# One shift row in the attention, the closing norm on VectorE, output weights loaded two ahead, and a new order for the start of the kernel

## The chip, the cores and the metric

One core of a Trainium2 chip runs the kernel. The time is that of one execution on the device in microseconds (us), from the first to the last instruction with what lies around them. Five engines work beside each other, each in the order of its own queue: PE (TensorE: matmuls and transposes; PEld are its weight loads), DVE (VectorE), ACT (ScalarE), POOL (GpSimd) and SP (SyncE, which here only issues transfers between HBM and the on-chip memory). Matmul results go to PSUM banks, everything else lives in SBUF tiles of 128 partitions. Before and after are compared by the median of several executions; one further execution was recorded by the profiler.

## The reference, cut to what matters

One layer, batch 1, 2048 positions, width 1024: an adaptive layer norm, an input projection, two branches (a gated linear recurrence and a forgetting attention of 8 heads of width 64), an output projection and a closing layer norm on the residual.

```python
mod = silu(c) @ w_ada + b_ada;  shift, scale, gate = split(mod, 3)
h = layer_norm(x) * (1 + scale) + shift
xr, zr, q, k, v, za, fl = split(h @ w_in)        # 6 of width 512, fl of width 8
y_r = rg_lru(causal_conv(xr))                    # gates by block matmuls, then a scan over positions
y_r = rms_norm(y_r, norm_lru) * silu(zr)
d = cumsum(log_sigmoid(fl + b_fgate))            # per head
s = q @ k.T / 8 + d[query] - d[key]              # causal
y_a = rms_norm(softmax(s) @ v, norm_attn) * silu(za)
y = concat(y_r, y_a) @ w_out
out = layer_norm(2 ** 0.25 * x + gate * y) * ln_gain + ln_bias
```

## The kernel before, in words

**Numbers.** Most operands are written as a sum of two f16 tiles (a high part, rounded on ACT, and the rest, on DVE or POOL), and a product is three f16 matmuls. The scales of these splits come from the largest absolute value of a tensor: `all_max` transposes column maxima on PE (`pam`), reduces them on DVE and spreads the result with a second small matmul. Every matmul is issued by the helper `mm` and therefore carries line L93; the tiles tell them apart.

**Input passes.** Positions are taken in four chunks of 512 (four tiles of 128). `load_x` loads a chunk, `norm_tile` normalises a tile: statistics and a few small steps on DVE (L236 to L244, one power on POOL), then the scaling in two halves on ACT (L266) and POOL (L268). *Pass 0* works through chunk 0 in eight steps k, one for each 128 of the width. In a step `scale_col` loads 128 columns of `w_ada` (`wadab`) and forms eight column matmuls with the activated `c` (`psc`), which give the scale of these 128 features; `load_w32` loads the matching rows of `w_in` (`wrow`) and rounds them (ACT L644, POOL L646); `make_h32` transposes the normalised x (`ptr`) and forms h in a high and a low part (ACT L380, DVE L381); `xr32` is twelve matmuls 128x512 into the four banks `pj` of the recurrence's input. *Pass 1* does the same with chunk 1, whose weights are there already, and beside it finds the scales for these weights (`col_max`, `xmax_fin`), splits them for f16 (`split_T`, tiles `wT`) and finds the shift of the adaptive norm (`wsh`, `va`, `pada`). *Pass 2* and *pass 3* take chunks 2 and 3 with the f16 weights (`make_hk`, `finish_h`, tiles `hf` and `hT`), add the shift's share to the earlier chunks (`xr_shift`: 16 small matmuls `pcj` for each of four column groups), and pass 3 prepares the weights of V (`vf_gen`: maxima, scales `vfr`, tiles `wN` and `wf`).

**Middle.** Then come V, the keys, the recurrence, the gates z and a, and the decay (`decay_gen`), each as matmuls over all chunks with element work on the other engines.

**Attention.** For each chunk of queries and each head (32 items) an item first finds a bound of the scores: matmuls `pmx` of the key rows kb (64 features, two constant rows, two rows of the decay, 68 in all) with the query rows qb, row maxima `mc` on DVE (L1259), a maximum over key blocks `mrow` (L1263). From it comes the shift of the query: L1267 writes `trow` in f32, L1268 rounds it into the f16 tile `Z`, L1269 writes the rest into the next column. PE transposes `Z` into `pzt` (66 rows), ACT copies the two rows to qb. Then for each block of keys: scores `pst` (two matmuls), exponent on ACT (L1290), split of the result into two f16 tiles (ACT L1292, then POOL L1294 or DVE L1296: `ph`), and the product with V into `acc`.

**Output.** `wout_gen` prepares the output weights beside the attention: it loads 128 rows (`woraw`), POOL multiplies them by the gate row `gbc` (L1003, 128x1024), ACT and DVE split them; one load is in flight ahead of the one at work. `out_gen` forms `pout` for a tile of positions whose attention is done, DVE adds the residual (`xres`, L1468), and `ln_gen` closes the tile: statistics on DVE, one scaling on ACT (L1385), gain and bias on POOL (L1387, L1388). The sixteenth tile has its own path (`out_last`, L1418 to L1429), which does gain and bias in four steps of 128x512 on DVE.

**What sets the order.** Each of these parts is a Python generator; the places of their `yield`s, `tick()` and `flush()` interleave them by hand. A scheduler then orders each engine's queue when the kernel is built; `tc.issue_after(ins)` adds an edge that it must keep. Buffers come from pools with fixed counts (`r4` eight of 4 KB, `t2` ten of 2 KB), so a load waits until the tile that held its buffer has been read.

Of the kernel before, what the change touches and what calls it, by code (L numbers as in the profile page):

```python
# [19 lines left out]
P = 128  # L20
# [18 lines left out]
def hybrid_mixer(  # L39
# [66 lines left out]
    kb = dr.tile([H, 68, S], F16, name="kb", tag="kb")  # L106
# [27 lines left out]
    def load_cols(parts, name):  # L134
        n = sum(k for _, k in parts)
        rows = t2([n, P], f"r_{name}")
        o = 0
        for ap, k in parts:
            flat = ap[0] if len(ap.shape) == 2 else ap[0].rearrange("k n -> (k n)")
            nc.scalar.dma_start(rows[o:o + k, :], flat.rearrange("(a b) -> a b", b=P))  # L140
# [53 lines left out]
    def pj_bank():  # L194
# [52 lines left out]
    def load_x(ci):  # L247
        xs = []
        for i in range(4):
# [5 lines left out]
            else:  # L255
                hv = [t2([P, CH], f"xt{g}") for g in range(2)]
                for g in range(2):
                    nc.sync.dma_start(hv[g], x[t * P:(t + 1) * P, g * CH:(g + 1) * CH])
# [86 lines left out]
    def split_h(ci, k, hf):  # L345
        a = nc.scalar.copy(hT(k, 0, ci), hf).ins
        nc.vector.tensor_tensor(hT(k, 1, ci), hf, hT(k, 0, ci), ALU.subtract)  # L347
# [316 lines left out]
    def wmax_fin():  # L664
        yield
        yield
        am = yield from all_max(wam, NW)
# [30 lines left out]
    def vf_gen(raws, fraw):  # L698
# [16 lines left out]
        nc.scalar.activation(wf[:, :, 0:H], fraw, AF.Copy, scale=rec[:, 1:2])  # L715
        nc.vector.scalar_tensor_tensor(wf[:, :, H:2 * H], fraw, rec[:, 1:2], wf[:, :, 0:H], ALU.mult, ALU.subtract)
# [15 lines left out]

    pss = [bank(t, "pj") for t in "AAAO"]
    for k in range(KT + 2):
# [12 lines left out]
        if k > 1:  # L747
            xr32(pss, 0, k - 2)
    xr32_out(pss, 0)
    pss = [bank(t, "pj") for t in "BBAA"]  # L750
    xam = cst([P, 4, KT], "xam")
# [11 lines left out]
    wu = []  # L763
    for k in range(KT + 2):
# [10 lines left out]
        if k == 4:  # L775
            chains.append(xmax_fin())
        if 2 <= k < 2 + 4:
            xraw.append(load_raw(P * len(xraw)))
        if k == 4:
            for g in range(2):  # L780
                nc.vector.tensor_tensor(va[g], va[g], pa[g], ALU.add)
        if k > 1:
            xr32(pss, 1, k - 2)
            tick()
        if k == 5:
# [10 lines left out]
            for j in range(4):  # L796
                wu.append((split_T(xraw[j], xrec[:, j:j + 1]), xun[:, j:j + 1]))
            norm_x(xs2, (1, 1, 1, 1,))
            last["pow2"] = last["pow"]
# [33 lines left out]
    new_h(3)  # L833
    for k in range(KT + 1):
# [11 lines left out]
        if k == 3:  # L846
            cs = [xr_shift(j) for j in range(4)]
        tick()
    flush()
# [6 lines left out]
    load_gates()  # L856
# [10 lines left out]
    nc.vector.memset(crow, RS)  # L867
    nc.scalar.dma_start(kb[:, DH:DH + 2, :].rearrange("h a s -> a h s"), crow.unsqueeze(1).broadcast_to([2, H, S]))
    QB = [cst([68, CH], f"qb{i}", F16) for i in range(4)]
    Z = [cst([P, 4, 68], f"Z{i}", F16) for i in range(4)]  # L870
    for q in QB:
        nc.scalar.dma_start(q[66:68, :], crow[:, 0:CH])
# [69 lines left out]
    def gate_gen():  # L942
# [7 lines left out]
        for k in range(KT):  # L950
# [5 lines left out]
            else:  # L956
                nc.gpsimd.tensor_tensor(out=acc, in0=acc, in1=w, op=ALU.add)
# [17 lines left out]
    def gate_fin(cols):  # L975
        yield
# [7 lines left out]
    def wout_gen():  # L984
# [15 lines left out]
        def wo_raw(k):  # L1000
            raw = r4([P, D], "woraw")
            nc.sync.dma_start(raw, w_out_v[k])
            nc.gpsimd.tensor_tensor(out=raw, in0=raw, in1=gbc, op=ALU.mult)  # L1003
            return raw

        nxt = wo_raw(0)
        yield
        for k in range(KT):
            raw = nxt
            if k + 1 < KT:  # L1010
                nxt = wo_raw(k + 1)
            w = wh([P, 2, D], "wo") if k < KT - 1 else r4([P, 2, D], "wo", F16)
            for n in range(2):
                sl = slice(n * CH, (n + 1) * CH)
                split_out(w[:, 0, sl], w[:, 1, sl], raw[:, sl], so[:, k:k + 1])
                yield
# [68 lines left out]
    def decay_gen():  # L1085
# [8 lines left out]
        yield  # L1094
        WT = t2([P, 2, H, TT], "WT")
# [28 lines left out]
        for h in range(H):  # L1124
            for a in range(2):
                nc.sync.dma_start(kb[h, DH + 2 + a, :].rearrange("(t p) -> t p", p=P), ndr[h * TT:(h + 1) * TT, a, :])
# [104 lines left out]
    def maxpass(ci, h, res):  # L1231
# [10 lines left out]
        nc.sync.dma_start(kk[0:68, 1, 0:nk], kb[h, :, 0:nk])  # L1242
# [3 lines left out]
        nc.gpsimd.memset(qb[DH:DH + 2, :], 0.0)  # L1246
# [3 lines left out]
        for i in range(4):  # L1250
            nk = (4 * ci + i + 1) * P
            for b in range(ci + 1):
# [3 lines left out]
                mm(ps[:, 0:w], qb[:, i * P:(i + 1) * P], kk[0:68, 1, b * CH:b * CH + w], True, not end)  # L1256
# [9 lines left out]
        t = sm([P, 4], "trow")  # L1266
        nc.vector.tensor_scalar(t, m, -1.0 / RS, ndc[:, ci, h:h + 1], ALU.mult, ALU.add)  # L1267
        nc.vector.tensor_copy(z[:, :, DH], t)  # L1268
        nc.vector.tensor_tensor(z[:, :, DH + 1], t, z[:, :, DH], ALU.subtract)  # L1269
# [349 lines left out]
```

## Time and profile before

| | |
|---|---|
| median of 3 runs | 1215.45 us (1214.27 to 1218.1) |
| profiled execution | 1211.64 us |
| its span, first to last instruction | 1209.9 us |
| mean granted TensorE clock | 0.966 |
| HBM read / written | 97.66 MB / 31.59 MB |

A row of the timeline gives start and length in us, engine, line, operation, output <- inputs, shape, count, and in brackets how long the engine had been idle and what ended that. In the groups the numbers behind a bar are busy us in all and mean ns of one. PSUM tiles begin with p (`pj`, `pst`, `pmx`, `pout`).

### The profile page before, as it was taken

The numbers are of one execution on the slowest core, as the hardware profiler recorded it, in microseconds if no ns is written. First come the engines' busy times: TensorE is split into PE (matmuls) and PEld (weight loads), VectorE is DVE, ScalarE is ACT, GpSimd is POOL, SyncE is SP. The second block draws the span as 40 slices with busy tenths as digits, with TensorE's granted clock in tenths as the row PEclk, the third lists the DMA queues.
The fourth block names the chain that finished last, engine by engine and source line by source line (L and its number), as shares of the span: only waits on it lengthen the run. The fifth ranks groups of instructions, "written<-read, shape, count | busy, mean of one in ns | idle before, by whom it ended". The sixth has DMA issues, their size and how long they took to land. (4 is left out here: it accounts for less than half of the span.)

```text
span 1209.9 us, 20217 instructions
## 1 busy us (share of the span) xinstructions
PE 1111.2 (92%) x7467; PEld 622.8 (51%) x7467; DVE 767.7 (63%) x1435; ACT 719.6 (59%) x1244; POOL 686.0 (57%) x670
## 2 busy tenths in 40 slices
PE   6997899999999899999979979989999989999787
PEld 6874444454444444434445545555565555565444
DVE  4378775766668953664396544576677677667534
ACT  3437545564758412623375657577888688888841
POOL 5715532444554300830277645687788689887854
PEclk9998989999999999999979989989999999999899
DMA  9653046221225712754063344222332233221001
GB/s 296 208 151 123 1 118 189 71 64 33 70 70 141 242 55 70 260 160 140 26 205 114 95 129 123 87 93 86 101 94 90 76 103 106 78 89 46 18 27 70
DMA packets 110248, 130.56 MB, mean 108 GB/s; under 512 B 10086, under 2 KB 79318, under 8 KB 110150
## 3 DMA queue, kind: packets, MB, share of 16 engines
q1 hardware_dynamic: 109840, 129.17, 35.0%
q8 instruction: 58, 0.95, 0.3%
q14 instruction: 40, 0.33, 0.1%
q10 hardware_dynamic: 310, 0.12, 0.0%
HBM read 97.66 MB, written 31.59 MB: 107 GB/s over the span
## 5 line engine op out<-in xcount | busy, mean ns | idle before, releaser
L93 PE MATMUL pj<-hT,wT 128*128 128x512 f16 x1440 | 324.4, 383 | 4.1 <-DVE hT L347 1.7
L1294 POOL TENSOR_TENSOR ph<-pf,ph 128x512 f16<-128x512 f32 (+2 forms) x240 | 260.5, 1100 | 67.4 <-ACT ph L1292 62.6
L93 PEld LDWEIGHTS <-wT 128*128 128x128 f16 x1792 | 169.2, 99 | 208.6 <-issue 21.6
L1259 DVE TENSOR_REDUCE mc<-pmx 128x1 f32<-128x512 f32 (+2 forms) x320 | 184.8, 603 | 114.2 <-PE pmx L93 110.0
L1290 ACT ACTIVATE pf<-pst,bias 128x512 f32<-128x512 f32 (+1 forms) x320 | 194.7, 634 | 66.4 <-PE pst L93 58.8
L1292 ACT CAST ph<-pf 128x512 f16<-128x512 f32 (+1 forms) x320 | 171.7, 569 | 20.1 <-PE acc L93 15.9
L93 PE MATMUL acc<-V,ph 128*128 128x129 f16 (+1 forms) x2176 | 158.6, 210 | 22.0 <-POOL ph L1294 14.6
L93 PEld LDWEIGHTS <-ph 128*128 128x128 f16 x2176 | 124.1, 99 | 80.6 <-POOL ph L1294 22.1
L93 PE MATMUL pst<-qs,kk 128*128 128x512 f16 (+1 forms) x320 | 114.3, 360 | 2.0 <-DVE mc L1259 1.3
L93 PE MATMUL pst<-qb,kk 66*128 66x512 f16 (+1 forms) x320 | 112.8, 362 | 0.2
L93 PE MATMUL pmx<-kk,qb 68*128 68x512 f16 (+2 forms) x320 | 105.0, 357 | 7.4 <-DMA kk<-kb 3.8
L93 PE MATMUL pout<-wo,yT 128*128 128x512 f16 (+1 forms) x396 | 95.7, 372 | 1.5 <-ACT yT L1370 1.5
L93 PE MATMUL pout<-wo,yr 128*128 128x512 f16 (+1 forms) x396 | 94.1, 381 | 2.8 <-DVE zs L1369 2.7
L93 PE MATMUL pj<-wN,hT 128*128 128x512 f16 x384 | 89.5, 378 | 0.2 <-ACT XL L814 0.2
L1188 POOL TENSOR_TENSOR XL<-XL,szr 128x512 f32<-128x512 f32 x16 | 24.3, 1522 | 114.7 <-ACT szr L1185 114.7
L1296 DVE TENSOR_TENSOR ph<-pf,ph 128x512 f16<-128x512 f32 (+1 forms) x80 | 64.3, 804 | 33.8 <-ACT ph L1292 33.2
L93 PEld LDWEIGHTS <-kk 66*128 66x128 f16 (+1 forms) x640 | 55.1, 100 | 34.5 <-issue 11.6
L93 PE MATMUL pq<-hT,wT 128*128 128x512 f16 x288 | 67.0, 379 | 2.8 <-DVE qhl L881 2.8
L93 PEld LDWEIGHTS <-hT 128*128 128x128 f16 x640 | 44.5, 97 | 48.3 <-issue 3.6
L93 PEld LDWEIGHTS <-yr 128*128 128x128 f16 x396 | 38.3, 100 | 42.8 <-issue 8.0
L93 PEld LDWEIGHTS <-yT 128*128 128x128 f16 x396 | 37.5, 98 | 39.4 <-ACT yT L1370 1.7
L483 POOL TENSOR_TENSOR xl<-xc,xh 128x512 fp32r<-128x512 f32 x16 | 24.4, 1532 | 57.8 <-ACT xh L481 47.0
(307 smaller groups left out, 1846.0 us busy)
## 6 DMA issues: line engine op xcount, KB each, us to landing
wraw<-in_w_in_dram SPq DMA_DIRECT2D x40, 512.0 KB
woraw<-in_w_out_dram SPq DMA_DIRECT2D x16, 512.0 KB
xres<-in_x_dram SPq DMA_DIRECT2D x16, 512.0 KB
out_dram<-xres SPq DMA_DIRECT2D x15, 512.0 KB
wadab<-in_w_ada_dram SPq DMA_DIRECT2D x8, 512.0 KB
xt<-in_x_dram SPq DMA_DIRECT2D x16, 256.0 KB
xt<-in_x_dram SPq DMA_DIRECT2D x8, 512.0 KB
wsh<-in_w_ada_dram SPq DMA_DIRECT2D x16, 256.0 KB
```

The source lines that it names most:

```text
L93: m = nc.tensor.matmul(o, lhsT=l, rhs=r, start=st, stop=sp, skip_group_check=chk)
L483: nc.gpsimd.tensor_tensor(out=xl, in0=xc, in1=xh, op=ALU.subtract)
L1188: nc.gpsimd.tensor_tensor(out=XL[j][:, sl], in0=XL[j][:, sl], in1=sz, op=ALU.mult)
L1259: nc.vector.tensor_reduce(out=mc[:, i, b:b + 1], in_=ps[:, 0:w], axis=AX.X, op=ALU.max)
L1290: nc.scalar.activation(pf32[:, 0:w], ps[:, 0:w], AF.Exp, scale=DH ** -0.5, bias=bias[:, ci, h, kt:kt + 1])
L1292: nc.scalar.copy(ph[:, 0, 0:w], pf32[:, 0:w])
L1294: nc.gpsimd.tensor_tensor(out=ph[:, 1, 0:w], in0=pf32[:, 0:w], in1=ph[:, 0, 0:w], op=ALU.subtract)
L1296: nc.vector.tensor_tensor(ph[:, 1, 0:w], pf32[:, 0:w], ph[:, 0, 0:w], ALU.subtract)
```

## The change

The start: x of chunk 0 is loaded ahead of the first weights, zeros are multiplied on PE (`spin`, 37 matmuls 128x512 in f16), and a dummy Silu stands ahead of the normalisation. The seven small vector loads go to SP's queue. In pass 0 a step issues its own `psc` and `ptr` and then the `xr32` of the step before; the column maxima of the weights move here from pass 1. In pass 1 the splits `wT` go one per step, the shift's matmuls one step earlier, and chunk 2 is normalised one tile per step from the seventh step on. In pass 3 the V weights are split with more yields between and `xr_shift` goes one per step.

```diff
+    warm = t2([P, CH], "warm", F16)
+    nc.vector.memset(warm, 0.0)
+    pw = bank("B", "pw")
+
+    def spin(n):
+        for _ in range(n):
+            with tc.issue_after(last["pe"]) if "pe" in last else ExitStack():
+                mm(pw, warm[:, 0:P], warm, True, True)
+
+    spin(12)
+    ccol = load_cols([(c, 8), (b_ada, 24)], "ada", nc.scalar)
...
+    swarm = sm([P, 1], "swarm")
+    nc.scalar.activation(swarm, epsc, AF.Silu)
...
+    spin(22)
+    for k in range(KT + 1):
         if k < KT:
-            scale_col(k)
-            load_w32(k)
-        if 0 < k <= KT:
-            make_h32(0, k - 1, xs)
+            with tc.issue_after(last["x0"]), tc.issue_after(last["pe"]):
+                scale_col(k)
+                load_w32(k)
+            with tc.issue_after(last["pe"]):
+                make_h32(0, k, xs)
+            if k == 0:
+                spin(3)
         if k == 4:
             xs1 = load_x(1)
...
-        if 6 <= k < 6 + 4:
-            norm_tile(xs1[k - 6], (1, 1, 1, 1,)[k - 6])
-        if k == KT:
...
-            xr32(pss, 0, k - 2)
+        if k > 0:
+            with tc.issue_after(last["pe"]):
+                xr32(pss, 0, k - 1)
+            with tc.issue_after(last["lo"]):
+                col_max(w32[k - 1][:, 0].rearrange("p (j n) -> p j n", n=P), AX.X, xam[:, :, k - 1])
...
-            for e in (2 * k, 2 * k + 1):
-                with tc.issue_after(last["lo"]):
-                    col_max(w32[e][:, 0].rearrange("p (j n) -> p j n", n=P), AX.X, xam[:, :, e])
+            xraw.append(load_raw(P * k))
         if k == 3:
...
+        tick()
+        if 3 <= k < 3 + 4:
+            with tc.issue_after(last["lo"]), tc.issue_after(hi_act[1, k]):
+                wu.append((split_T(xraw[k - 3], xrec[:, k - 3:k - 2]), xun[:, k - 3:k - 2]))
+        if k == 4:
...
-            norm_x(xs2, (1, 1, 1, 1,))
-            last["pow2"] = last["pow"]
+        if k >= 6:
+            norm_tile(xs2[k - 6], 1)
+    last["pow2"] = last["pow"]
...
-        if k == 3:
-            cs = [xr_shift(j) for j in range(4)]
         tick()
+        if 3 <= k < 7:
+            cs.append(xr_shift(k - 3))
```

On SP's queue, at its very start, before and then now (`wrow`, `wadab`: the weights of a step; `xt`: halves of x):

```order
L642 DMA wrow_223<-in_w_in_dram 128x512
L632 DMA wadab_211<-in_w_ada_dram 128x8x128
L632 DMA wadab_228<-in_w_ada_dram 128x8x128
L258 DMA xt0_139<-in_x_dram 128x512
L258 DMA xt1_140<-in_x_dram 128x512
L258 DMA xt0_143<-in_x_dram 128x512
```

```order
L265 DMA xt0_144<-in_x_dram 128x512
L265 DMA xt1_145<-in_x_dram 128x512
L265 DMA xt0_148<-in_x_dram 128x512
L265 DMA xt1_149<-in_x_dram 128x512
L265 DMA xt0_152<-in_x_dram 128x512
L265 DMA xt1_153<-in_x_dram 128x512
L265 DMA xt0_156<-in_x_dram 128x512
L265 DMA xt1_157<-in_x_dram 128x512
L639 DMA wadab_239<-in_w_ada_dram 128x8x128
L649 DMA wrow_251<-in_w_in_dram 128x512
```

Three weight loads stood ahead of x; now all eight halves of x stand ahead of every weight.

On PE, near the end of pass 3, before and then now (`pam`: the spreading of the V maxima that the V scales need; `pcj`: shift columns; `ptr`: transposes of the last chunk):

```order
L93 MATMUL pcj_1390<-B16_127,wT_802 128x2
L93 LDWEIGHTS wT_802
L93 MATMUL pcj_1390<-B16_127,wT_802 128x1
L93 MATMUL pam_1292<-amd_1296,ones_78 128x2
L390 MATMUL ptr_1432<-ident_69,xt_931 128x128
L390 MATMUL ptr_1432<-ident_69,xt_933 128x128
```

```order
L93 MATMUL pj_1249<-hT30_1252,wT_879 128x512
L93 MATMUL pam_1338<-amd_1342,ones_78 128x2
L93 LDWEIGHTS wT_784
L93 MATMUL pcj_1379<-B16_132,wT_784 128x2
L93 LDWEIGHTS wT_784
L93 MATMUL pcj_1379<-B16_132,wT_784 128x1
```

The matmul of the V maxima stood behind the last group of shift columns; now it stands ahead of the first.

Attention and output: one of the two constant rows of kb and one of the two shift rows of qb go, and the shift is written straight into `Z` in f16. (The shift is the same for all keys of a query, so its rounding cancels in the softmax.) `wout_gen` keeps two loads in flight and multiplies in halves, `ln_gen` closes a tile with four steps on DVE. A few generators get more yields, and the gate sum `acc` goes in halves.

```diff
-    kb = dr.tile([H, 68, S], F16, name="kb", tag="kb")
+    kb = dr.tile([H, 67, S], F16, name="kb", tag="kb")
...
-        nxt = wo_raw(0)
-        yield
+        def wo_gate(raw):
+            for n in range(2):
+                sl = slice(n * CH, (n + 1) * CH)
+                nc.gpsimd.tensor_tensor(out=raw[:, sl], in0=raw[:, sl], in1=gbc[:, sl], op=ALU.mult)
+
+        raws = [wo_raw(0), wo_raw(1)]
+        yield
+        wo_gate(raws[0])
         for k in range(KT):
-            raw = nxt
-            if k + 1 < KT:
-                nxt = wo_raw(k + 1)
+            raw = raws.pop(0)
             w = wh([P, 2, D], "wo") if k < KT - 1 else r4([P, 2, D], "wo", F16)
             for n in range(2):
                 sl = slice(n * CH, (n + 1) * CH)
                 split_out(w[:, 0, sl], w[:, 1, sl], raw[:, sl], so[:, k:k + 1])
+                if n == 0 and k + 2 < KT:
+                    raws.append(wo_raw(k + 2))
+                if n == 0 and k + 1 < KT:
+                    wo_gate(raws[0])
                 yield
             wo.append(w)
...
-        t = sm([P, 4], "trow")
-        nc.vector.tensor_scalar(t, m, -1.0 / RS, ndc[:, ci, h:h + 1], ALU.mult, ALU.add)
-        nc.vector.tensor_copy(z[:, :, DH], t)
-        nc.vector.tensor_tensor(z[:, :, DH + 1], t, z[:, :, DH], ALU.subtract)
+        nc.vector.tensor_scalar(z[:, :, DH], m, -1.0 / RS, ndc[:, ci, h:h + 1], ALU.mult, ALU.add)
...
-        nm = sm([P, 1], "nm")
-        nc.vector.scalar_tensor_tensor(nm, mv[:, 0:1], -1.0, rs, ALU.mult, ALU.mult)
-        nc.scalar.activation(xt, xt, AF.Identity, scale=rs, bias=nm)
-        yield
-        nc.gpsimd.tensor_tensor(out=xt, in0=xt, in1=late["lng"], op=ALU.mult)
-        nc.gpsimd.tensor_tensor(out=xt, in0=xt, in1=late["lnb"], op=ALU.add)
+        for n in range(2):
+            ns = slice(n * CH, (n + 1) * CH)
+            nc.vector.scalar_tensor_tensor(xt[:, ns], xt[:, ns], mv[:, 0:1], late["lng"][:, ns], ALU.subtract, ALU.mult)
+            yield
+        for n in range(2):
+            ns = slice(n * CH, (n + 1) * CH)
+            nc.vector.scalar_tensor_tensor(xt[:, ns], xt[:, ns], rs, late["lnb"][:, ns], ALU.mult, ALU.add)
+            if n == 0:
+                yield
         nc.sync.dma_start(out[tt * P:(tt + 1) * P, :], xt)
```

On DVE, at one item of the attention, before and then (at another item) now (`mc`, `mrow`: score maxima; `Z`: the shift; `xres`: a tile in its closing norm):

```order
L1259 TENSOR_REDUCE mc<-pmx 128x1 x2
L1263 TENSOR_REDUCE mrow<-mc 128x4
L1296 TENSOR_TENSOR ph<-pf_6333,ph 128x512
L1267 TENSOR_SCALAR trow<-mrow,ndc 128x4
L1268 CAST Z_1610<-trow 128x4
L1269 TENSOR_TENSOR Z_1610<-trow,Z_1610 128x4
```

```order
L1300 TENSOR_REDUCE mrow_8943<-mc_8743 128x4
L1414 BN_AGGR mv_8971<-bst_8716 128x2
L1303 TENSOR_SCALAR Z3_1657<-mrow_8943,ndc_3580 128x4
L1430 TENSOR_SCALAR ve_8973<-mv_8971 128x1
L1419 SCALAR_TENSOR_TENSOR xres_8057<-xres_8057,mv_8971,lng_7088 128x512 x2
L1423 SCALAR_TENSOR_TENSOR xres_8057<-xres_8057,rs_8975,lnb_7090 128x512
L1505 SCALAR_TENSOR_TENSOR xres_8590<-pout_9017,kap_1668,xres_8590 128x512
```

Three small steps from the maximum to `Z` became one, and four steps of 128x512 for a tile's closing norm stand among the maxima.

More of the change, by code (lines that the diff above doesn't have):

```diff
@@ L257, in load_x @@
                 for g in range(2):
[L258 removed]
+                    last[f"x{ci}"] = nc.sync.dma_start(hv[g], x[t * P:(t + 1) * P, g * CH:(g + 1) * CH]).ins
             xs.append(hv)
@@ L346, in split_h @@
         a = nc.scalar.copy(hT(k, 0, ci), hf).ins
-        nc.vector.tensor_tensor(hT(k, 1, ci), hf, hT(k, 0, ci), ALU.subtract)
+        last["hlo"] = nc.vector.tensor_tensor(hT(k, 1, ci), hf, hT(k, 0, ci), ALU.subtract).ins
         return a
@@ L666, in wmax_fin @@
         yield
-        am = yield from all_max(wam, NW)
+        am = yield from all_max(wam, NW, 3)
         scales(am, RS, winv, wrec)
@@ L714, in vf_gen @@
             wv.append(w)
-        nc.scalar.activation(wf[:, :, 0:H], fraw, AF.Copy, scale=rec[:, 1:2])
-        nc.vector.scalar_tensor_tensor(wf[:, :, H:2 * H], fraw, rec[:, 1:2], wf[:, :, 0:H], ALU.mult, ALU.subtract)
+            yield
+            if q == 2:
+                nc.scalar.activation(wf[:, :, 0:H], fraw, AF.Copy, scale=rec[:, 1:2])
+                nc.vector.scalar_tensor_tensor(wf[:, :, H:2 * H], fraw, rec[:, 1:2], wf[:, :, 0:H],
+                                               ALU.mult, ALU.subtract)
+                for _ in range(2):
+                    yield
     xs = load_x(0)
@@ L769, in hybrid_mixer @@
         if k < 4:
-            for e in (2 * k, 2 * k + 1):
-                with tc.issue_after(last["lo"]):
-                    col_max(w32[e][:, 0].rearrange("p (j n) -> p j n", n=P), AX.X, xam[:, :, e])
+            xraw.append(load_raw(P * k))
         if k == 3:
             xs2 = load_x(2)
[L775 to L781, printed above, removed]
+            with tc.issue_after(last["lo"]):
+                for g in range(2):
+                    nc.vector.tensor_tensor(va[g], va[g], pa[g], ALU.add)
         if k > 1:
             xr32(pss, 1, k - 2)
-            tick()
-        if k == 5:
+        tick()
[3 more added lines that the diff above has]
+        if k == 4:
             flush()
@@ L855, in hybrid_mixer @@
     nc.scalar.dma_start(bfg, b_fgate[0].partition_broadcast(P))
-    load_gates()
+    with tc.issue_after(hi_act[3, KT - 1]), tc.issue_after(last["hlo"]):
+        load_gates()
     sp = sm([P, 4], "sp")
@@ L866, in hybrid_mixer @@
     crow = r4([2, S], "crow", F16)
-    nc.vector.memset(crow, RS)
-    nc.scalar.dma_start(kb[:, DH:DH + 2, :].rearrange("h a s -> a h s"), crow.unsqueeze(1).broadcast_to([2, H, S]))
-    QB = [cst([68, CH], f"qb{i}", F16) for i in range(4)]
+    with tc.issue_after(last["hlo"]):
+        nc.vector.memset(crow, RS)
+    nc.scalar.dma_start(kb[:, DH:DH + 1, :].rearrange("h a s -> a h s"), crow[0:1].unsqueeze(1).broadcast_to([1, H, S]))
+    QB = [cst([67, CH], f"qb{i}", F16) for i in range(4)]
     Z = [cst([P, 4, 68], f"Z{i}", F16) for i in range(4)]
     for q in QB:
-        nc.scalar.dma_start(q[66:68, :], crow[:, 0:CH])
+        nc.scalar.dma_start(q[65:67, :], crow[:, 0:CH])
     for z in Z:
@@ L956, in gate_gen @@
             else:
-                nc.gpsimd.tensor_tensor(out=acc, in0=acc, in1=w, op=ALU.add)
+                for n in range(2):
+                    sl = slice(n * CH, (n + 1) * CH)
+                    nc.gpsimd.tensor_tensor(out=acc[:, sl], in0=acc[:, sl], in1=w[:, sl], op=ALU.add)
             if k % 2 == 1:
```

48 lines of the change are left out of this document (27 added, 21 removed).

## The prediction

> **What bounds the kernel now.** First the page: its span and the engines' totals.
>
> ```profile
> span 1209.9 us, 20217 instructions
> ...
> PE 1111.2 (92%) x7467; PEld 622.8 (51%) x7467; DVE 767.7 (63%) x1435; ACT 719.6 (59%) x1244; POOL 686.0 (57%) x670
> ```
>
> PE is busy 92% of the span, and nothing in the diff takes real matmuls away. So a gain can only come from PE's idle time, 1209.9 - 1111.2 = 98.7 us, and from matmuls that ran below full clock. The view by windows, cut where the stages change, says where both lie. Columns after the window: its length, then busy us of PE, PEld, DVE, ACT and POOL, then the clock, DMA share and GB/s.
>
> ```profile
> 0.00:65.00 65.00, 52.74 (x268) 46.90 (x269) 28.28 (x73) 27.90 (x43) 42.74 (x53) 1.00 0.83 255
> 65.00:106.00 41.00, 32.77 (x158) 25.39 (x157) 31.13 (x76) 17.55 (x26) 8.39 (x13) 0.92 0.51 165
> 106.00:170.00 64.00, 57.33 (x388) 30.80 (x388) 51.02 (x98) 41.86 (x67) 35.91 (x32) 0.89 0.21 53
> 170.00:600.00 430.00, 414.97 (x2088) 198.05 (x2087) 268.88 (x439) 203.16 (x271) 152.71 (x106) 0.99 0.38 112
> 600.00:850.00 250.00, 220.58 (x1717) 126.66 (x1715) 154.50 (x327) 166.84 (x343) 168.92 (x195) 0.92 0.39 117
> 850.00:1120.00 270.00, 261.42 (x2345) 154.72 (x2342) 196.99 (x367) 219.63 (x418) 220.54 (x224) 0.99 0.27 86
> 1120.00:1203.00 83.00, 71.36 (x517) 40.28 (x515) 32.97 (x58) 42.67 (x81) 55.76 (x49) 0.94 0.09 33
> ```
>
> Idle time of PE: 12.3, 8.2 and 6.7 us in the three front windows (27.2), 15.0 in the middle, 29.4, 8.6 and 11.6 in attention (49.6). The middle is PE-bound and the change hardly touches it. Two places decide: the four input passes and attention. In attention the view of waits names what PE waits for (total us, times, longest):
>
> ```profile
> PE acc L93 <- POOL ph L1294: 14.6, 20, 3.5
> PE pzt L93 <- DVE Z L1269: 9.1, 10, 2.3
> ```
>
> **Pass 0.** The timeline of PE's input matmuls (start, length, count) shows the first two steps of pass 0, its last group, and the transition from pass 1 to pass 2:
>
> ```profile
> 28.62 5.47 PE L93 MATMUL pj<-h,w 128*128 128x512 f32 x12
> 33.89 0.85 PE L379 MATMUL ptr<-ident,xt 128*128 128x128 f32 x4
> 34.49 2.99 PE L93 MATMUL pj<-h,w 128*128 128x512 f32 x12
> 37.32 0.95 PE L93 MATMUL psc<-cact,wadab 128*128 128x1 f32 x8
> ...
> 61.27 3.00 PE L93 MATMUL pj<-h,w 128*128 128x512 f32 x12
> ...
> 91.23 3.01 PE L93 MATMUL pj<-h,w 128*128 128x512 f32 x12 [1.00 <-ACT h L380]
> ...
> 105.90 1.09 PE L93 MATMUL pj<-hT,wT 128*128 128x512 f16 x4
> ```
>
> Before, the first 12 input matmuls start at 28.62, behind 24 column matmuls of later steps, and the last of pass 0 end at 61.27 + 3.00 = 64.27. After, x is loaded ahead of the weights and each step issues its own 8 column matmuls, 4 transposes and the 12 of the step before. What then starts the first group is the normalisation of x, one tile after another on DVE:
>
> ```profile
> 8.58 1.38 DVE L236 BATCH_NORM_STATS2 bst<-xt 128x6 f32<-128x512 f32 x2 [2.65 <-DMA xt<-in_x_dram]
> ...
> 16.12 1.28 DVE L236 BATCH_NORM_STATS2 bst<-xt 128x6 f32<-128x512 f32 x2
> ```
>
> Four tiles at (16.12 - 8.58)/3 = 2.5 us. The last one's statistics end at 17.4; some 2 us to its normalised half, and 2 more for transposes and the two halves of h put the first group at 21.5 if x lands no sooner, at 18.5 if x lands 3 us sooner (what 1.25 MB ahead of it take at the 255 GB/s of the first window is 4.9 us, so 3 is the cautious part). I take 20. From there eight groups of 3.0 and seven pairs of columns and transposes, 0.95 + 0.60 each (the transposes from start to start, 34.49 - 33.89), are 34.9 us: pass 0 ends at 55 if PE never waits, and I allow 1 us of waits: 55.8 instead of 64.3, **-8.5** (bounds -5 and -11). The column matmuls that moved behind the start cost PE nothing more, since each runs once either way. The eight column maxima of the weights move on DVE from pass 1, where DVE is 31.1 of 41 us busy, to pass 0, where it is 28.3 of 65. SP's queue gets the seven small vector loads in place of ACT's; they stand among the loads of x of chunk 1 and hold the weights of step 5 up by seven issues, covered by the four steps of 4.6 us before it. The 37 matmuls on zeros run while PE has nothing: 37 at 0.47 us (a half-clock group of the same shape, quoted below, has 4 in 1.86) are 17 us at worst, and so end before 20. Cost nothing; if they outlast the first h, +2.
>
> The clock: the group at 28.62 took 5.47, the next 2.99, so half rate costs the first group 2.5 us. [...]
>
> **From pass 1 to pass 2.** The last group of pass 1 ends at 91.23 + 3.01 = 94.24, the next input matmul is at 105.90: 11.7 us, in which DVE, ACT and PE bring four tiles of chunk 2 through their statistics one by one (2.5 us each, as above). After, tiles 0 and 1 are normalised within pass 1, so that two tiles of 2.5 and the tail of about 2 remain: 7.2, **-4.5** (bounds 0, if DVE has no room for them in pass 1, and -7). The splits that went one per step instead of four at once change DVE's order only; ±1.
>
> **Pass 3.** PE's timeline:
>
> ```profile
> 141.35 2.75 PE L93 MATMUL pj<-hT,wT 128*128 128x512 f16 x12
> ...
> 154.00 1.86 PE L93 MATMUL pj<-hT,wT 128*128 128x512 f16 x4 [0.24 <-ACT hT L346]
> ...
> 161.78 5.34 PE L93 MATMUL pj<-hT,wT 128*128 128x512 f16 x24
> ```
>
> Between 144.10 and 154.00 PE does the four groups of shift columns and 16 transposes, and then runs 4 matmuls in 1.86 where 24 take 5.34 (0.22 each): half clock until about 161.8. The V scales come out of a sum that in PE's order stood behind all shift groups; now it stands ahead of them, with the shift groups one per step. The hole loses some 5 of its 9.9 us, and with it most of the half clock, worth (161.8 - 154)/2 = 3.9: **-8** (bounds -2 and -10). Pass 2 gets back what its DVE must now do later: +0.5. Waits added here (the gate loads behind the last h, yields in the scale generators) lie in the PE-bound middle, where 15 us of idle in 430 are spread: **-1** (±3).
>
> **Attention.** Rows of the removed and of the added work (count, then ns of one, least/median/most, then first and last start; in the last row busy us and mean ns):
>
> ```profile
> L1268 DVE CAST Z<-trow x32: 164/178/1134, 590.3 to 1129.8; 128x4 f16<-128x4 f32 x32
> L1269 DVE TENSOR_TENSOR Z<-trow,Z x32: 170/179/2359, 590.5 to 1130.9; 128x4 f16<-128x4 f32 x32
> ```
>
> ```profile
> L1387 POOL TENSOR_TENSOR xres<-xres,lng x15: 2346/2356/2387, 763.6 to 1196.6; 128x1024 f32<-128x1024 f32 x15
> L1388 POOL TENSOR_TENSOR xres<-xres,lnb x15: 2342/2347/2371, 767.9 to 1199.0; 128x1024 f32<-128x1024 f32 x15
> ```
>
> ```profile
> L1427 DVE SCALAR_TENSOR_TENSOR xres<-xres,mv,lng x2: 745/746/748, 1204.3 to 1204.9; 128x512 f32<-128x512 f32 x2
> ```
>
> ```profile
> L1296 DVE TENSOR_TENSOR ph<-pf,ph 128x512 f16<-128x512 f32 x48 | 49.5, 1031 | 20.3 <-ACT ph L1292 20.0
> ```
>
> The shift: two of three DVE steps on the way to PE's transpose go. Their medians are 0.18 us, but single ones took 1.1 and 2.4; the 9.1 us that PE waits for Z should fall to about 3: **-6**. Output weights two ahead: one load came late and POOL stood before it, and all of attention behind POOL:
>
> ```profile
> 704.27 2.34 POOL L1003 TENSOR_TENSOR woraw<-woraw,gbc 128x1024 f32<-128x1024 f32 x1 [7.65 <-DMA woraw<-in_w_out_dram]
> ```
>
> ```profile
> 707.29 0.56 PE L93 MATMUL acc<-V,ph 128*128 128x65 f16 x5 [3.53 <-POOL ph L1294]
> ```
>
> Of the other 11.1 us of PE's waits for this step of POOL I count 2.5 to the same stall: 6 us, now gone: **-6** (bounds +3, if the third buffer that it now holds keeps a key load back, and -9). Its multiplication in two halves keeps POOL's other work waiting half as long, and the key rows, 67 for 68, cost PE nothing, as its time goes by columns; both 0. Closing norm: POOL loses 15 x (2.356 + 2.347) = 70.5 us, DVE gains 60 x 0.746 = 44.8 us, a price from the tail, where nothing runs beside it. L1296, two tensors of the same shape among POOL's steps, averages 1.03, so I take that in attention: 62 us, against two short steps saved at each Z. What a long POOL step does to DVE now:
>
> ```profile
> 1130.92 2.27 DVE L1269 TENSOR_TENSOR Z<-trow,Z 128x4 f16<-128x4 f32 x1
> ```
>
> ```profile
> 1130.81 2.35 POOL L1388 TENSOR_TENSOR xres<-xres,lnb 128x1024 f32<-128x1024 f32 x1
> ```
>
> Both end within 0.03 us: a 0.18 us step sat through the whole POOL step, and PE behind it. Those stalls go (**-3**), and with fewer holes the clock of 0.92 over 220 us rises a little (**-4**). In their place 60 steps stand on DVE ahead of the score maxima and Z: I put **+5**, a twelfth of a microsecond each, since DVE is 73% busy from 850 to 1120 and PE's queue runs ahead. Bounds: 0, and 62 if PE waits for each in full. Sum for attention -14.
>
> [...]
>
> **Sum.** -8.5 - 4.5 - 8 + 0.5 - 1 - 14 = -35.5. The profiled run took 1211.64, so 1176.1; it lies 3.8 under the median of the runs, 1215.45, so **1180**.
>
> **Rivals.**
> - Front only: DVE becomes what attention waits for and eats its 19 us of gains (0.3 us per added step): 1180 + 14 = 1194. For it: maxima and L1296 sit on DVE behind the new pairs. Against: DVE idles 27% there.
> - Slower: each added step holds Z or a maximum that PE waits for. The other terms give 21.5 in front and middle and 19 in attention, 40.5; from (40.5 + 3.6)/60 = 0.74 us per step, its whole length, the kernel is measurably slower (0.3%, 3.6 us, is about what a measurement of it can tell from no change). At 1.03 each: 62 - 40.5 = +21.5, 1237. Only if PE is never ahead; its 97% in 850 to 1120 says that it is.
> - The front doesn't come: x first makes the weights late, the holes move by a step and the clock is cold anyway. Then -15 remain: 1200.
> - More: attention gets half of its 49.6 us of idle time back, and all front bounds hold: 1160.
>
> **How the numbers follow.** Forecast (1170 to 1190) 0.52, front only 0.16, front missing 0.10, more 0.09, effects cancelling to within 0.3% 0.05, slower 0.08. Leaving out 2 in 10, half at each end: 1160 to 1208. Faster 0.87, same 0.05, slower 0.08.
>
> **What would show it.** The first 12 input matmuls near 20 us and 3.0 long; pass 2's first f16 matmul 7 us behind pass 1's last; no half-clock groups near 150; no wait for output weights in POOL's row; the wait for Z near 3 us. It would be wrong if the new DVE steps average over 1.1 us, if PE's waits for DVE in attention grow past 20 us, or if pass 0 still begins after 25.

## The result: slower, and where the time went

The changed kernel takes 1271.55 us in the median of 4 runs (1269.71 to 1276.52), beside 1214.86 us of the kernel before (4 runs): ratio 1.0469, 95% interval 1.0424 to 1.0513. The forecast was 1180, with 1208 as its upper end. The profiled execution took 1271.1 us, its span is 1269.0.

The page of the changed kernel, span and engine totals:

```profile
span 1269.0 us, 20286 instructions
...
PE 1122.3 (88%) x7504; PEld 623.0 (49%) x7504; DVE 777.9 (61%) x1417; ACT 711.0 (56%) x1234; POOL 626.9 (49%) x655
```

PE has 11 us more work (the zeros, and a mean granted clock of 0.938, not 0.966), but 147 us of idle time instead of 99. The windows, cut at the same times as those of before up to 1120:

```profile
0.00:65.00 65.00, 61.88 (x327) 48.02 (x328) 35.84 (x92) 29.40 (x46) 42.45 (x53) 0.92 0.88 273
65.00:106.00 41.00, 36.67 (x182) 26.16 (x181) 30.33 (x69) 26.46 (x40) 13.35 (x18) 0.92 0.41 133
106.00:170.00 64.00, 59.75 (x389) 31.52 (x388) 42.69 (x81) 35.59 (x57) 28.82 (x26) 0.95 0.15 39
170.00:600.00 430.00, 409.87 (x2124) 198.08 (x2123) 280.73 (x467) 216.71 (x295) 158.82 (x123) 0.98 0.41 120
600.00:850.00 250.00, 203.86 (x1545) 116.13 (x1544) 131.25 (x256) 145.23 (x301) 145.12 (x180) 0.88 0.31 95
850.00:1120.00 270.00, 220.16 (x1912) 128.54 (x1911) 167.83 (x304) 174.37 (x337) 158.66 (x174) 0.91 0.24 81
```

The front has less idle time than before, 12 us instead of 27, though the zeros, 11.07 us of work in the first window, fill most of the difference. Attention has far more: 46 us instead of 29 in the fifth window, 50 instead of 9 in the sixth, and all engines are less busy there, DVE and POOL too. So no engine became the bound; all wait for something else. The view of PE's waits names it (total us, times, longest):

```profile
PE pout L93 <- DVE zs L1403: 44.7, 6, 19.0
PE pmx L93 <- DMA kk<-kb: 29.0, 5, 7.9
PE acc L93 <- POOL ph L1328: 15.2, 23, 3.7
PE pzt L93 <- DVE Z L1303: 6.1, 4, 2.5
```

The first two in the kernel before:

```profile
PE pmx L93 <- DMA kk<-kb: 3.8, 3, 1.5
PE pout L93 <- DVE zs L1369: 2.7, 3, 1.4
```

Both are transfers, since DVE's step on `zs` itself waits for the load of `zs`:

```profile
DVE zs L1403 <- DMA zs<-zd: 50.8, 5, 19.3
```

The longest of PE's waits, 19.0 us, ends at 1074.63. SP's queue just ahead of it (start, length of the issue):

```profile
1032.05 0.43 SPq L1278 DMA_DIRECT2D kk<-kd  x1
1032.52 0.73 SPq L1279 DMA_DIRECT2D kk<-kb  x1
1033.30 0.60 SPq L1278 DMA_DIRECT2D kk<-kd  x1
1033.94 0.62 SPq L1279 DMA_DIRECT2D kk<-kb  x1
1034.61 10.85 SPq L1278 DMA_DIRECT2D kk<-kd  x1
1045.51 1.09 SPq L1279 DMA_DIRECT2D kk<-kb  x1
1046.70 10.73 SPq L1383 DMA_DIRECT2D xres<-in_x_dram  x1
1057.47 1.20 SPq L1380 DMA_DIRECT2D zs<-zd  x1
```

In the kernel before nine in ten of attention's issues take 0.3 to 0.6 us and none over 1.5; here two take over 10. What the transfers do meanwhile is in the last two columns of a view by windows of 3 us (the share of the 16 DMA engines that is busy, GB/s):

```profile
1039.00:1042.00 3.00, 3.00 (x16) 1.42 (x15) 0.84 (x3) 2.42 (x5) 2.57 (x3) 1.00 0.10 34
1042.00:1045.00 3.00, 3.00 (x31) 1.79 (x29) 3.00 (x4) 2.51 (x4) 1.81 (x2) 1.00 0.06 26
...
1048.00:1051.00 3.00, 3.00 (x35) 1.96 (x32) 0.69 (x1) 2.95 (x7) 2.35 (x3) 1.00 0.07 30
1051.00:1054.00 3.00, 3.00 (x34) 2.03 (x33) 2.43 (x5) 2.19 (x6) 0.86 (x2) 1.00 0.06 26
```

A share of 0.06 is one engine of 16, at 26 GB/s. A load of `kb` for the last chunk is 67 rows of 4 KB, 268 KB or 274,000 bytes: 10.5 us at that rate, which is what the two long issues took. So the loads issued later seem to stand behind the key rows on that one engine. With 68 rows, in the kernel before, a load of `kb` is issued at 903.33, nothing else on SP's queue until 909.94, and when the load of `kd` ahead of it has drained the share stands at about a quarter, four engines of 16:

```profile
906.00:908.00 2.00, 2.00 (x24) 1.50 (x25) 1.82 (x4) 2.00 (x5) 2.00 (x4) 1.00 0.27 107
```

On how many engines a load of 64 rows runs is not shown here. The change took one row away and with it three of four engines.

### The profile page after: what moved, and what is told of

It reads as the page before. It is cut to its first block, busy times and chain, and to the rows that moved or that the text cites. A ratio compares the mean times of both kernels' runs of the same rounds, so it can differ in the third digit from the quotient of the medians.

```text
span 1269.0 us, 20286 instructions
## 1 busy us (share of the span) xinstructions
PE 1122.3 (88%) x7504; PEld 623.0 (49%) x7504; DVE 777.9 (61%) x1417; ACT 711.0 (56%) x1234; POOL 626.9 (49%) x655
## 5 line engine op out<-in xcount | busy, mean ns | idle before, releaser
L1328 POOL TENSOR_TENSOR ph<-pf,ph 128x512 f16<-128x512 f32 (+2 forms) x240 | 266.7, 1124 | 110.4 <-ACT ph L1326 98.9
L93 PE MATMUL pout<-wo,yr 128*128 128x512 f16 (+1 forms) x396 | 99.5, 399 | 44.7 <-DVE zs L1403 44.7
L93 PE MATMUL pmx<-kk,qb 67*128 67x512 f16 (+2 forms) x320 | 106.6, 366 | 33.4 <-DMA kk<-kb 29.0
L93 PE MATMUL pst<-qb,kk 65*128 65x512 f16 (+1 forms) x320 | 113.4, 363 | 0.1
L1330 DVE TENSOR_TENSOR ph<-pf,ph 128x512 f16<-128x512 f32 (+1 forms) x80 | 59.9, 748 | 40.7 <-ACT ph L1326 39.7
L93 PEld LDWEIGHTS <-kk 65*128 65x128 f16 (+1 forms) x640 | 55.1, 100 | 47.4 <-issue 24.9
L93 PE MATMUL pq<-hT,wT 128*128 128x512 f16 x288 | 70.3, 396 | 0.6 <-DVE qhl L906 0.6
L93 PE MATMUL pj<-h,w 128*128 128x512 f32 x192 | 52.3, 423 | 0.8 <-ACT h L387 0.8
```

Source lines behind the costliest of these rows:

```text
L93: m = nc.tensor.matmul(o, lhsT=l, rhs=r, start=st, stop=sp, skip_group_check=chk)
L1328: nc.gpsimd.tensor_tensor(out=ph[:, 1, 0:w], in0=pf32[:, 0:w], in1=ph[:, 0, 0:w], op=ALU.subtract)
L1330: nc.vector.tensor_tensor(ph[:, 1, 0:w], pf32[:, 0:w], ph[:, 0, 0:w], ALU.subtract)
```

## The experiments

"Before" in each line is the kernel before in runs on the same chip. Ratios carry their 95% interval.

| run | median us | before | ratio |
|---|---|---|---|
| e1_split64 | 1189.91 | 1217.13 | 0.9794 (0.9747 to 0.9841) |
| e2_rows68 | 1203.01 | 1217.13 | 0.9888 (0.9832 to 0.9944) |
| e3_before67 | 1293.58 | 1217.13 | 1.0652 (1.0591 to 1.0713) |
| e4_split64_oldnorm | 1188.43 | 1217.13 | 0.9777 (0.9726 to 0.9827) |
| e5_before64 | 1214.19 | 1218.53 | 0.9964 (0.9933 to 0.9994) |
| e6_nozeros | 1189.37 | 1218.53 | 0.9759 (0.9731 to 0.9786) |
| e7_before_oneshift | 1200.66 | 1218.53 | 0.9868 (0.9833 to 0.9902) |
| e8_before_wo2 | 1230.54 | 1218.53 | 1.0109 (1.0074 to 1.0144) |
| e9_best | 1182.00 | 1218.07 | 0.9710 (0.9683 to 0.9737) |
| e10_best_halves | 1185.22 | 1218.07 | 0.9722 (0.9682 to 0.9761) |
| e11_front | 1221.70 | 1218.07 | 1.0024 (1.0003 to 1.0045) |
| e12_best_oldnorm | 1180.22 | 1218.07 | 0.9689 (0.9662 to 0.9716) |
| e13_yield | 1225.96 | 1216.33 | 1.0080 (1.0044 to 1.0116) |
| e14_best_noyield | 1189.00 | 1216.33 | 0.9784 (0.9747 to 0.9821) |
| e15_front_noyield | 1213.72 | 1216.33 | 0.9992 (0.9965 to 1.0019) |

### The load of the key rows, alone

Changed kernel, the load in 64 and 3 rows (e1):

```diff
-        nc.sync.dma_start(kk[0:67, 1, 0:nk], kb[h, :, 0:nk])
+        nc.sync.dma_start(kk[0:DH, 1, 0:nk], kb[h, 0:DH, 0:nk])
+        nc.sync.dma_start(kk[DH:67, 1, 0:nk], kb[h, DH:67, 0:nk])
```

> The changed kernel, but a head's key rows kb (67 of them) are loaded as 64 rows and 3 rows instead of 67 at once. Theory A (a transfer of 67 rows runs on one of the 16 DMA engines: in the changed kernel's trace the DMA share stands at 0.06 and 25 GB/s for stretches of ten us behind such a load): the 72.8 us that attention lost come back with most of what was forecast for it; 1175 to 1195 us, PE's waits for kb and zs under 10 us instead of 73.7. Rival B (the output store waits on SP's queue for the closing norm, now on VectorE, 182 us instead of 106, and holds the key loads behind it): no more than a third comes back, over 1245.

Changed kernel, 68 rows in HBM and in the load, row 67 filled with the constant and read by no matmul (e2):

```diff
-    kb = dr.tile([H, 67, S], F16, name="kb", tag="kb")
+    kb = dr.tile([H, 68, S], F16, name="kb", tag="kb")
...
-        nc.sync.dma_start(kk[0:67, 1, 0:nk], kb[h, :, 0:nk])
+        nc.sync.dma_start(kk[0:68, 1, 0:nk], kb[h, :, 0:nk])
```

> The changed kernel with kb padded back to 68 rows in HBM (row 67 filled with the constant, read by no matmul) and loaded as 68 rows at once. Theory A: 68 can be shared by 4 engines, as before, so about 1180 to 1200, at most 10 us behind the load in 64 and 3. If it is the bytes or the number of loads that count, not the row number, it stays above 1250. Rival B: above 1245.

Kernel before, its 68 rows in 67 and 1 (e3):

```diff
-        nc.sync.dma_start(kk[0:68, 1, 0:nk], kb[h, :, 0:nk])
+        nc.sync.dma_start(kk[0:67, 1, 0:nk], kb[h, 0:67, 0:nk])
+        nc.sync.dma_start(kk[67:68, 1, 0:nk], kb[h, 67:68, 0:nk])
```

> The kernel before with nothing changed but the load of kb's 68 rows: 67 rows and 1 row. Theory A: 32 loads of 67 to 268 KB at some 26 GB/s instead of four times that, so 60 to 90 us slower than before, 1275 to 1305, with stretches of DMA share 0.06. Rival B (closing norm and SP's order): the kernel before, 1211 to 1222.

Kernel before, its 68 rows in 64 and 4 (e5; the diff as in e1, with 68 for 67):

> The kernel before with only the load of kb's 68 rows split into 64 and 4. [...]

Measured: with 64 and 3 rows the changed kernel falls from 1271.55 to 1189.91, by 82 us; with 68 rows to 1203.01, by 69 us. In that run (e2) the four engines hold attention's instructions in the same order as in the changed kernel, so there the row number alone has changed. The kernel before, with nothing but its load cut at 67 and its four engines in the same order too, rises by 76 us, to 1293.58. The waits of e1 and of e3, first rows of each:

```profile
PE acc L93 <- POOL ph L1329: 8.7, 18, 0.8
PE pmx L93 <- DMA kk<-kb: 8.6, 2, 5.7
```

```profile
PE pout L93 <- DVE zs L1370: 36.1, 6, 15.9
PE acc L93 <- POOL ph L1295: 29.3, 21, 12.8
PE pmx L93 <- DMA kk<-kb: 16.9, 3, 6.0
```

In e1 the wait for `zs` has left the head of the list (1.9 us); in e3 it has come into a kernel that hardly had it, and a window of its trace shows the single engine:

```profile
1009.00:1012.00 3.00, 3.00 (x39) 2.04 (x38) 1.27 (x2) 1.94 (x5) 0.09 (x1) 1.00 0.06 25
```

Made and unmade, with everything else in place: this is the cause. It is not the number of loads either, since e3 and e5 both cut the load of the kernel before in two, and only the cut at 67 costs time. The rival, output stores that hold SP's queue while they wait for the norm on DVE, is out: that wait is 182.3 us in the changed kernel and still 175.8 in e1, which is 82 us faster. e5 is 4 us faster than before (0.9964). Its engines run the same attention in the same order as before, so about 4 us (1 to 8 by the interval) is what 64 and 4 rows give over 68 at once; the 13 us between e1 and e2, whose orders differ at 120 of attention's 4670 matmuls, are not all the load's.

### The closing norm

e1 with the norm of the kernel before (e4):

```diff
-        for n in range(2):
...
-            nc.vector.scalar_tensor_tensor(xt[:, ns], xt[:, ns], rs, late["lnb"][:, ns], ALU.mult, ALU.add)
...
+        nc.scalar.activation(xt, xt, AF.Identity, scale=rs, bias=nm)
+        yield
+        nc.gpsimd.tensor_tensor(out=xt, in0=xt, in1=late["lng"], op=ALU.mult)
+        nc.gpsimd.tensor_tensor(out=xt, in0=xt, in1=late["lnb"], op=ALU.add)
```

> The load in 64 and 3 rows as in the first run, with the closing norm as in the kernel before (ACT, then two steps of 128x1024 on POOL). By the prediction's terms the norm on VectorE is worth some 3 to 5 us net (POOL stalls gone 3, clock part of 4, cost 5), so this run lies within 8 us of the first. By rival B, and by the forecast's own rival of VectorE as the bound, this run is 10 us or more faster than the first.

1188.43 against 1189.91: no difference that these runs can tell. The 10 us of the rivals are out. The 3 to 5 us of the prediction are not told apart from nothing, all the more as 2104 of attention's 4670 matmuls stand at another place in the two.

### The zeros

e1 without them (e6):

```diff
-    spin(12)
...
-    spin(22)
...
-            if k == 0:
-                spin(3)
```

> The changed kernel with the load in 64 and 3 rows and without the 37 matmuls on zeros. In the changed kernel the first group of twelve still took 4.95 us, as at half clock, although the zeros ran until 11.8. Theory: the zeros bought nothing, the first group starts at 19 to 20 and the time is within 4 us of the run with zeros (1189.9). Rival: they kept the clock up for the columns and transposes ahead of it; then 3 to 6 us slower.

1189.37 against 1189.91: in the time they buy nothing and cost nothing. Within pass 0 they do both. Without them the first group starts at 21.20, not at 19 to 20 as expected and not at 19.46 as in e1, because 16 column matmuls ahead of it take 3.54 us instead of 1.92. But the fourth group takes 3.02 us, where it takes 4.61 in e1.

### One shift row, and the output weights, each alone in the kernel before

The shift in one step, the second row left at zero (e7):

```diff
-        t = sm([P, 4], "trow")
-        nc.vector.tensor_scalar(t, m, -1.0 / RS, ndc[:, ci, h:h + 1], ALU.mult, ALU.add)
-        nc.vector.tensor_copy(z[:, :, DH], t)
-        nc.vector.tensor_tensor(z[:, :, DH + 1], t, z[:, :, DH], ALU.subtract)
+        nc.vector.tensor_scalar(z[:, :, DH], m, -1.0 / RS, ndc[:, ci, h:h + 1], ALU.mult, ALU.add)
```

> The kernel before with only the shift formed in one VectorE step instead of three; the second shift row stays in place and holds zero, the key rows stay 68. The prediction's term: 6 us faster, PE's wait for Z 3 us instead of 9.1. Rival (PE waits for the next thing instead): within 3 us of before, with the wait for Z lower all the same.

Output weights two ahead and multiplied in halves, as in the change (e8: `wout_gen` of the changed kernel in the kernel before):

> The kernel before with only the output weights loaded two ahead and multiplied in halves. The prediction's term: 6 us faster, no wait of POOL for the weights' load. Rival (the third buffer holds key loads back, or PE waits elsewhere): within 3 us of before, or slower, with PE's wait for kk above 3.8 us.

e7 is 18 us faster, three times the term; PE's wait for Z falls nearly as expected:

```profile
PE pzt L93 <- DVE Z L1266: 3.7, 3, 1.9
```

e8 is 12 us slower, where 6 us of gain were expected. PE meets a new wait in its trace:

```profile
699.27 0.58 PE L93 MATMUL pmx<-kk,qb 68*128 68x512 f16 x1 [7.56 <-DMA kk<-kb]
```

and the waits of SP's queue between 687 and 695 say for what that key load had stood:

```profile
SPq L1248 <- POOL woraw L1008: 5.6, 1, 5.6
```

The multiplications in that trace:

```profile
L1008 POOL TENSOR_TENSOR woraw<-woraw,gbc x16: 1261/1265/2247, 607.5 to 692.8; 128x512 f32<-128x512 f32 x16
```

The key load is issued at 694.07, just behind the last of them. What that step sets free is the gate row `gbc`; the weights themselves are read by ACT and DVE only after it. So the key load stood for the buffer of `gbc`, which is in the same pool, and the addresses in the built kernel agree. In the kernel before a key load waits for the same buffer, 4.4 us in SP's queue, but there it is a later load that has been given it. The third set of weights in flight has shifted the buffers by one.

PE's waits for the keys rise from 3.8 to 10.0 us in all, as the rival had it. POOL's waits for the weights do fall, from 14.3 to 3.3, but PE's wait for `ph` from POOL, out of which the term took its 6 us, stays at 14.5 (14.6 before). That leaves half of the 12 us without a wait of its own; attention's order is another too, in more than 1800 of the 4670 matmuls.

### What is left, put together

e1 with the output weights of the kernel before (e9), the same with the multiplication in halves (e10), and e9 with the norm of the kernel before (e12):

```diff
+            nc.gpsimd.tensor_tensor(out=raw, in0=raw, in1=gbc, op=ALU.mult)
...
-        raws = [wo_raw(0), wo_raw(1)]
+        nxt = wo_raw(0)
         yield
-        wo_gate(raws[0])
         for k in range(KT):
-            raw = raws.pop(0)
+            raw = nxt
+            if k + 1 < KT:
+                nxt = wo_raw(k + 1)
...
-                if n == 0 and k + 2 < KT:
-                    raws.append(wo_raw(k + 2))
-                if n == 0 and k + 1 < KT:
-                    wo_gate(raws[0])
```

> The changed kernel with the load in 64 and 3 rows and the output weights as in the kernel before (one ahead, one multiplication of 128x1024). Two ahead alone made the kernel before 12 us slower, with a wait of 7.6 us for key rows that sat behind the third buffer. Theory: the same here, so 8 to 14 us under the run with 64 and 3 rows (1189.9): 1176 to 1182. Rival (that cost was due to the load on 4 engines, and the split has taken it away): within 4 us of 1189.9.

> As the run before it in this list, but with the multiplication in two halves. If the cost of the edit lies in the second load ahead, this run is within 4 us of the run with one multiplication; if it lies in the halves (two steps on POOL's queue and another order), within 4 us of 1189.9.

> As the first run of this list, with the closing norm on ACT and POOL as in the kernel before. With the output weights two ahead the norm's place made no difference (1188.4 against 1189.9). Theory: again within 4 us of the first run of this list. Rival: with POOL no longer held up elsewhere the norm on VectorE is worth 5 us or more.

1182.00 for e9, 8 us under e1, as the theory had it, so the second load ahead seems to cost time here too (e14 below weakens this). e10 at 1185.22 lies between and is not told apart from either. e12, at 1180.22, is the fastest kernel run, though not told apart from e9: 3.1% under the kernel before (2.8 to 3.4), 7% under the changed one. The norm's place again makes no difference.

### The start and the passes alone

The changed kernel with attention, output weights and norm of the kernel before, 68 key rows (e11):

> The changed kernel with attention, output weights and closing norm as in the kernel before (68 key rows, three steps for the shift): the new start and the new order of the passes and the middle alone. The prediction's terms for these are 21.5 us; the traces show attention beginning 13 to 14 us earlier. Theory: that is all of it, 12 to 16 us faster than before. Rival (it is given back in attention): within 5 us of before.

1221.70, no faster than before, though its attention begins at 574.9 and that of before at 584.5: with the same work it takes 21 us longer in the profiled runs (574.9 to 1214.4, against 584.5 to 1202.6), some 13 by the medians. The two orders differ in 1768 of attention's 4670 matmuls, and a difference of nearly that size comes from one line of the change, a yield in the decay generator:

```diff
                                        ALU.min, ALU.subtract)
         yield
+        yield
```

The kernel before with that line alone (e13), e9 without it (e14), and e11 without it (e15):

> The kernel before with one more yield in the decay generator, which is one line of the change, and nothing else. It adds no work, but the scheduler then lays attention out in another order: by the rows of the two orders, 1762 of the 4670 matmuls of attention stand at another place. Theory D (this order is worse by itself): 12 to 22 us slower than before. Rival (the start and the middle give their gain back through something else, such as loads that meet): within 4 us of before.

> The kernel with the load in 64 and 3 rows and the output weights one ahead (1182.0), without that yield. There the yield moves 2 of the 4670 matmuls, since the other edits already set another order. Theory D: no difference, within 4 us of 1182.0. Rival (the yield costs time through what it delays, whatever the order): 8 us or more faster.

> The run with the new start and the new order of passes and middle alone (1221.7), without that yield; 75 of attention's matmuls then stand elsewhere than in the kernel before, not 1768. Theory D: attention takes its 612 us again and the gain of the start arrives at the end: 10 to 16 us faster than before. Rival: as with the yield, within 5 us of before.

e13: 10 us slower, a little less than expected, for a line that adds no work. Its attention begins at 584.5 as before and ends 14 us later in the profiled run (1216.7 against 1202.6), so the loss lies there, with the order. In e15 8 us are back against e11, but 1213.72 against 1216.33 is still no measurable gain (0.9965 to 1.0019). Its middle stage takes 423 us from the first V matmul to attention where before it takes 415; the windows of e15 and of the kernel before from V to attention, each from its own trace:

```profile
152.00:575.00 423.00, 404.39 (x2023) 191.77 (x2020) 275.11 (x447) 204.19 (x270) 145.97 (x109) 0.98 0.41 121
```

```profile
169.00:584.00 415.00, 400.51 (x1989) 190.25 (x1990) 262.66 (x419) 197.66 (x263) 148.74 (x102) 0.99 0.39 115
```

So of 17 us at V 9 reach attention. The last 9 are lost within attention, from 575.4 to the last output matmul at 1202.6 in e15, 584.5 to 1202.6 before. The two orders are close enough there to lay beside each other: e15 leads by 9.1 us until 606 on the clock of the kernel before and is level with it at 655. In that stretch (595 to 664 in e15, 604 to 664 before) PE waits 5.6 us for Z instead of 1.6, and its clock is 0.83 instead of 0.89. Why Z comes later there is open; e15's order still differs in 75 matmuls, and the profiled run of before was 4 us under its median.

e14 was expected to change nothing and is 7 us slower than e9. Attention is not where: 2 of its 4670 matmuls stand elsewhere, and it takes 600 us in e14 and 602 in e9. But it begins at 575.9 instead of 567.9. In the middle the same matmuls run 3.7 us later from 440 on (by e9's clock) and 8.0 later from 512 on, and e14 has a wait there that e9 has not:

```profile
PE pcs L93 <- DVE lfT L1121: 2.5, 1, 2.5
```

`lfT` is formed just ahead of the yield, so the yield has a use of its own besides the order: it gives DVE the time for that step. The rival, what it delays, was the nearer guess, with the other sign. How the 2.5 us become 8 is not shown. By its ratio e14, with the output weights one ahead, is no faster than e1 with two ahead, so the price of the second load ahead in the changed kernel is not settled. And since the order of attention alone moves the time by 10 us (e13), no verdict here that rests on 8 us or less between kernels with different orders is firm.

## Why the prediction was wrong, point by point

**The start of pass 0** was right in its mechanism and brought three fifths of its size. The changed kernel's input matmuls on PE, first, fourth and last group of pass 0, then the transition to pass 2, then V:

```profile
19.46 4.95 PE L93 MATMUL pj<-h,w 128*128 128x512 f32 x12 [0.76 <-ACT h L387]
...
36.57 4.60 PE L93 MATMUL pj<-h,w 128*128 128x512 f32 x12
...
56.19 3.02 PE L93 MATMUL pj<-h,w 128*128 128x512 f32 x12
...
84.68 2.98 PE L93 MATMUL pj<-h,w 128*128 128x512 f32 x12
...
95.21 5.36 PE L93 MATMUL pj<-hT,wT 128*128 128x512 f16 x16
...
153.96 16.35 PE L93 MATMUL pj<-wN,hT 128*128 128x512 f16 x75
```

The first group starts at 19.46 (forecast 20). It takes 4.95, as if no zeros had run, and the group at 36.57 is slow again, so pass 0 ends at 59.2, not 55.8: 5.1 us of the 8.5. Some 2.5 of the 8.5 stood for a first group of 3.0 instead of 5.47; without them the forecast would have been 6, which is nearer. The granted clock, by windows of 1 us, is 1.00 up to 16, 0.50 from 17 to 23 and again from 38 to 40. In the kernel before it reads 1.00 from 28 to 34, over the group that took 5.47, so the half rate of that group is read off its length alone. What brings the clock down here is not shown: 34 of the zeros end at 11.80 and the last three at 15.57, and from 11.80 to the first group PE is never idle for more than 0.82 us. It does column matmuls and transposes there, as it does ahead of the group at 36.57. That these don't hold the clock up would fit; no run tries it.

**From pass 1 to pass 2**: 87.66 to 95.21 is 7.6 us, forecast 7.2. Right.

**Pass 3**: V begins at 153.96 and before at 169.4, so 15.4 us of the front's 20.5 are there; pass 2 and 3 brought 4.7 where 7.5 were forecast. The hole behind the shift columns is smaller, not gone: 8.0 us from the last `pj` ahead of them (132.62) to the next (140.66), where it was 9.9. The mechanism was right, the sizes a quarter too large.

**The middle**, priced at -1, lost some 2 us in the changed kernel (attention 13.6 us early) and 8 in e15. That the added waits cost next to nothing because PE is busy there was the wrong argument: a yield in the decay generator, which the prediction doesn't name, changes the order of attention, worth 10 us (e13).

**The step that failed** is the one put in half a sentence: "the key rows, 67 for 68, cost PE nothing, as its time goes by columns; both 0". PE's time is the same with 67 rows: the `pmx` matmuls take 0.379 us in the median with 68 and with 67. But the row number also changed how many engines carry the load (a DMA share of 0.27 with 68, of 0.06 with 67), and that was never priced, in the sum or in a rival: no edit to a transfer's shape was read as an edit to a transfer. Against 68 rows at once it costs 69 us here (e2) and, as 67 and 1, 76 in the kernel before (e3), against 64 and 3 rows 82 (e1, with a slightly different order). The prediction's own sign of being wrong, PE's waits for DVE past 20 us, did show (44.7 us for `zs`), but DVE was waiting there for a load itself.

**The output weights** (-6) had the wrong sign: +12 alone (e8), and no gain in the changed kernel (e9 and e14 against e1). The step that failed is that PE's wait for `ph` would go with POOL's wait for the weights; it stayed at 14.5. The bound "+3, if the third buffer that it now holds keeps a key load back" came nearest: a key load is held back, by the gate row's buffer, and PE's waits for keys grew by 6.2 us.

**The shift** (-6) had the right sign and a third of its size: -18 in e7. The wait for Z fell from 9.1 to 3.7, 5.4 of the forecast's 6. Attention's order is another as well, in more than 1200 of the 4670 matmuls; that the other 12 us come from it is likely after e13, but not shown.

**The closing norm** came to nothing, as the sum of its three terms nearly said (+5, -3 and part of -4). Its steps in the changed kernel, by groups (busy us, mean ns of one):

```profile
L1423 DVE SCALAR_TENSOR_TENSOR xres<-xres,rs,lnb 128x512 f32<-128x512 f32 x30 | 33.8, 1155 | 0.4 <-POOL rs L1432 0.4
...
L1419 DVE SCALAR_TENSOR_TENSOR xres<-xres,mv,lng 128x512 f32<-128x512 f32 x30 | 26.7, 929 | 0.0
```

Together they are busy for 60.5 us, 1.01 a step, and last 1.04 in the mean, priced at 1.03. The forecast's slower rival, these steps in PE's way, was not what happened: without the load on one engine the same steps stand in a kernel of 1189.91. Whether steps of DVE and POOL hold each other up, as the pair of rows in the prediction suggests (2.27 us for a DVE step of 0.18 in the median, beside a POOL step of 2.35), e4 doesn't settle.

**The sum.** Without the one-engine load the changed kernel is 27 us faster than before, where 35.5 were forecast. That this is near is luck, as the terms were off both ways: shift -18 for -6, output weights +12 for -6, norm 0 for some -2, start and middle +4 to -3 for -21.5. Nor do the single runs add up to 27: all but the load's row number change the order of attention, and the order alone is worth 10 us.

## What to carry to other kernels

Whenever an edit changes the shape of a transfer, by a single row too, look up its DMA share in a trace, and where the share is low try the load in two parts: 64 and 3 rows took 82 us less than 67 here, while 67 and 1 took 76 us more than 68. A prefetch one deeper takes its buffer from someone: see who shares the pool before calling it free. And where a scheduler sets the order, try an edit without work (a yield) first; what it changes is the size below which no edit's verdict can be trusted.

## What the runs showed of the hardware that was not expected

- A load of 67 rows moves at 25 to 26 GB/s with a DMA share of 0.06; issues behind two of them took 10.85 and 10.73 us instead of 0.3 to 0.6, and a `zs` load issued at 1057.47 let DVE start on it at 1073.9.
- A load of 68 rows moves at 107 GB/s with a share of 0.27. Cutting it into 64 and 4 rows (e5) is worth 4 us, cutting it into 67 and 1 (e3) costs 76.
- Ten microseconds of matmuls on zeros, ended 7.7 us ahead of the first group, and three more, ended 3.9 us ahead, left that group at 4.95 us, near the 5.47 of before. The granted clock read 0.50 from 17 to 23; from the 34th of the zeros to the first group PE had no gap over 0.82 us. Leaving the zeros out did not change the time (e6).
